# The MLP of a decoder layer by one level of Strassen's algorithm: 7 block products for 8, with the sums of weight blocks on GpSimd

## The chip, the cores and the metric

The kernel runs on one core of a Trainium2 chip. The time is device microseconds of one execution; the median of three runs of the kernel before is 1074.55 us (1074.43 to 1076.7). The engines are named as in the profile: PE multiplies matrices (PEld is its load of weights), DVE, ACT and POOL work element by element on 128 partitions, SP issues the DMAs. PE writes its results to PSUM; DVE, ACT and POOL keep theirs in SBUF.

## What is computed

One step of a two-branch decoder layer on 512 prompt tokens and 8 sample tokens. The change concerns its last part, the MLP and what surrounds it:

```
x = x + g1 * (merged @ w_out)                       # w_out: 1024 x 1024
h2 = rmsnorm(x, norm2_g) * (1 + sc2) + sh2
ff = square(relu(h2 @ w_ff1)) @ w_ff2               # w_ff1: 1024 x 4096, w_ff2: 4096 x 1024
x = x + g2 * ff
y = rmsnorm(x, final_norm_g)
```

Scale, shift and gate (sc2, sh2, g2) come from a conditioning vector; the prompt has one and each sample its own. Everything is float32.

## The kernel before

Activations lie as features x tokens: a tile is 128 features by T = 520 columns, 512 of the prompt and 8 of the samples, and its two halves of 260 columns (HALF) go to PE one after the other. A tile of weights is 1024 rows x 128 columns. PE's format fp32r carries fewer bits than float32, so every operand is split in two parts, hi and lo: ACT casts it to hi (L68 for weights, L146 for activations), and DVE subtracts hi from it, which gives lo (L69, L147). A product is then three: hi hi, hi lo and lo hi (`products`, L100, 128 x 128 weights and 260 columns each).

The MLP runs over two halves of 2048 inner features. In each half, 16 tiles of the first product (8 blocks of 128 input features, 3 parts, 2 halves of the tokens: 48 matmuls a tile) are evacuated by DVE and ACT, squared, split and kept; then 8 output tiles of the second product (16 blocks, 96 matmuls a tile) are added to x by DVE (`residual`). These are 2 x 16 x 48 + 2 x 8 x 96 = 3072 matmuls.

The second norm's root is not waited for: `out_proj` multiplies x by 1 + sc2 and splits it for each of the eight output tiles of w_out, and the products begin on that. The shifts ride along as ten more columns of the second half (260 + 10 = 270), and `norm2` computes the root of the mean square meanwhile; L891 multiplies the products by it as it reads them from PSUM. The last output tile is computed half by half of the tokens (`last_tile`), so that the final norm of the first half lies beside the products of the second.

The order on every engine is set by the tile framework's scheduler from priorities and its own estimates; each engine then takes its instructions in that order. A weight tile comes by one DMA of 512 KB from SP's queue into one of four buffers (`wst`), and is split two tiles ahead of its use (AHEAD). POOL has next to nothing to do in the MLP.

Of the kernel before, what the change touches and what calls it, by code (L numbers as in the profile page):

```python
# [22 lines left out]
C = 128          # HGRN2 chunk  # L23
# [9 lines left out]
MODK = 7         # the product behind which a conditioning tile's transposes come  # L33
LEAD = 4         # first conditioning tiles ahead of the normed input's
# [4 lines left out]
T2 = T + NM + 1  # columns with the shifts beside the activations  # L39
# [6 lines left out]
class Kernel:  # L46
# [6 lines left out]
    # ---- weights: a tile is 1024 rows x 128 columns, in two parts that fp32r carries exactly  # L53
# [21 lines left out]
    def take_w(self, key):  # L75
# [18 lines left out]
    def products(self, ps, w, a, first, last, extra=0, halves=(0, 1)):  # L94
        """ps += W^T a, for one 128 x 128 tile of W and one tile of a, both in two parts."""
        (wh, wl), (ah, al) = w, a
        for n, (x, y) in enumerate(((wh, ah), (wh, al), (wl, ah))):
            for s in halves:
                c = slice(s * HALF, (s + 1) * HALF + s * extra)
                self.last_product = self.nc.tensor.matmul(ps[:, s, :c.stop - c.start], x, y[:, c],  # L100
                                                          start=first and n == 0, stop=last and n == 2)

    def gemm(self, keys, acts, extra=0):
        """[128, 2, HALF (+ extra in the second)] of W^T act for one tile of 128 output features."""
        ps = self.pmm.tile([128, 2, 512], F32, name="mm")
        for q, key in enumerate(keys):
            hi, lo = self.take_w(key)
            for k in range(KO):
                n = q * KO + k
                self.products(ps, (hi[:, k], lo[:, k]), acts[n], n == 0, n == len(keys) * KO - 1, extra)  # L110
# [4 lines left out]
    # ---- ScalarE's tables: what needs the exponential's and the root's stays together between sigmoids  # L115
# [34 lines left out]
    def rsqrt_small(self, x, n, p=128, w=16):  # L150
        """x[p, n] ** -0.5 to float32's accuracy (x normal and positive)."""
# [12 lines left out]
    # ---- constants and parameters  # L164
# [36 lines left out]
    def transpose_in(self, out, rows, n):  # L201
        """rows [n, 128] -> out [128, n]"""
# [8 lines left out]
    def bounds(self):  # L211
        """What depends on parameters through the exponential: HGRN2's lower bounds, RG-LRU's decay rates."""
# [7 lines left out]
        # lower bounds: softmax and exclusive cumsum over the one layer  # L220
# [17 lines left out]
    def decays(self):  # L238
        """c8 = 8 softplus(-lam); log1p(e) = 2 atanh(e / (2 + e))"""
# [15 lines left out]
    def parameters_mod(self):  # L255
        """The norms' scales and the conditioning's bias (plus one where a scale comes of it)."""
# [44 lines left out]
    # ---- conditioning  # L301
# [9 lines left out]
    def cond(self):  # L311
        """silu of the conditioning rows, transposed, with room for 32 of them."""
# [56 lines left out]
    # ---- the input, its norm, and its transpose  # L369
# [8 lines left out]
    def norm_x(self):  # L378
# [3 lines left out]
        junk = lambda: self.pmm.tile([128, 2, 512], F32, name="mm").rearrange("p a b -> p (a b)")  # noqa: E731  # L382
# [20 lines left out]
    def transposed(self, k):  # L403
        """Columns k * 128 .. + 128 of the rows, transposed where they are."""
# [15 lines left out]
    def affine_split(self, k, prompt, sample):  # L420
        """The normed input's tile k times 1 + scale, plus the shift, in two parts."""
# [7 lines left out]
        v = lambda t: t[:, :L].rearrange("p (t f) -> p t f", f=128)  # noqa: E731  # L429
# [4 lines left out]
    # ---- HGRN2  # L434
# [9 lines left out]
    def head_f(self, h, ps):  # L444
        """f = max(lb, floor) + (1 - lb) sigmoid(fa), k = (1 - lb) sigmoid(-fa)"""
# [43 lines left out]
    def head_sample_v(self, h, v):  # L489
# [3 lines left out]
        vs = self.sm.tile([NB, 128], F32, name="vs")  # L493
# [8 lines left out]
    def head_sample(self, h, st, vb, fkq):  # L502
# [5 lines left out]
        # four samples' states at a time, each with all samples' queries in its own 32 columns of the array  # L508
# [4 lines left out]
        ev = self.sm.tile([128, 256], F32, name="sev")  # L513
# [7 lines left out]
    def head_prompt(self, h, f, X, q, v, og):  # L521
        nc = self.nc
        # values as [s, v]
# [6 lines left out]
        # levels: Q_b[t] = q_t * f's from the b-block's start to t, K_b[s] = k_s * f's after s to the block's end,  # L530
        # T_b = the product of f over each b-block; a pair in neighbouring blocks 2i, 2i + 1 is K_b . Q_b
# [4 lines left out]
        a32 = self.sm.tile([128, NC, 32], F32, name="a32")  # L536
# [10 lines left out]
        def view(t, first_q, first_k, step, n, b):  # L547
            """n blocks of b columns, step apart, of Q from first_q on and of K from first_k on"""
# [616 lines left out]
```

## Time and profile before

| | |
|---|---|
| median of three runs | 1074.55 us |
| profiled execution, first to last instruction (its span) | 1070.9 us |
| median of the runs less that span | 3.65 us |
| from the first product of w_ff1 to the last of w_ff2 | 681.8 to 1061.0 us of the span |
| matmuls there | 3072 of 10132 on PE |

The execution that was profiled has no time of its own beside its span, so what lies around the span is taken from the median. The profile gives the busy time of each engine, the same in 40 slices of the span, the chain of work that ended last, and groups of instructions by line: `L69 DVE TENSOR_TENSOR wlo<-wst,whi 128x1024 ... x152 | 185.6, 1221` is line 69 on DVE, with the tile it writes and those that it reads, 152 instructions, 185.6 us in all and 1221 ns of one.

### The profile page before, as it was taken

Reading aid. Unit: us, or ns where it says so; the run is one execution under the profiler, and the core shown is the slowest. Engines: PE = TensorE matmul, PEld = TensorE weight load, DVE = VectorE, ACT = ScalarE, POOL = GpSimd, SP = SyncE. Lnnn points to the kernel's source line nnn. Section 1 sums busy time; section 2 is a strip of 40 time slices with the busy share of each in tenths; the row PEclk is TensorE's granted clock in tenths of the full one; section 3 lists DMA queues with packets and bytes.
Section 4 is the critical chain, followed back from the end, with each engine's and each line's share of the span. In section 5 each row is a group of like instructions: output and inputs, shape, how many; then the busy total and the mean of one; then the engine's idle time right before and its main releaser. Section 6 shows DMA issues by size and latency. Waiting matters only on the chain.

```text
span 1070.9 us, 23934 instructions
## 1 busy us (share of the span) xinstructions
PE 1035.1 (97%) x10132; PEld 998.7 (93%) x10132; DVE 603.9 (56%) x1429; ACT 446.8 (42%) x897; POOL 25.6 (2%) x68
## 2 busy tenths in 40 slices
PE   3899999999999999989999999999999999999996
PEld 1799999999999999989999999999999999999996
DVE  6568678596786867464333346665542235554333
ACT  5445744663574364351222234444421124443332
POOL 2200000000000000110000000000000000000000
PEclk9999999999999999999999999999999999999999
DMA  9953444334333324695555573333323333332312
GB/s 278 252 170 101 121 123 125 111 121 141 107 120 113 110 92 142 186 281 165 160 158 160 158 210 86 92 90 89 94 84 99 85 94 93 86 96 82 96 44 80
DMA packets 239212, 136.34 MB, mean 127 GB/s; under 512 B 5214, under 2 KB 233750, under 8 KB 239098
## 3 DMA queue, kind: packets, MB, share of 16 engines
q1 hardware_dynamic: 237218, 129.75, 42.3%
q0 software_dynamic: 1888, 5.07, 1.5%
q8 instruction: 79, 1.29, 0.5%
q14 instruction: 27, 0.22, 0.1%
HBM read 123.61 MB, written 11.26 MB: 126 GB/s over the span
## 4 chain that ended last, share of the span: by engine, by line
PE 93%; SPq 3%; DMA 2%; ACT 1%; DVE 1%; issue 0%; ACTq 0%; DVEq 0%
PE mm L100 82%; PE ps L339 2%; SPq L1061 2%; PE pb L685 1%; DMA wst<-in_w_in_dram 1%; PE ps L544 1%; DMA wm<-in_w_mod_dram 1%; PE pt L628 1%; PE pt L617 1%; SPq L62 1%; PE ps L512 1%; PE pt L630 1%; PE ps L582 0%; PE pt L611 0%; DMA vd<-vs 0%
## 5 line engine op out<-in xcount | busy, mean ns | idle before, releaser
L100 PE MATMUL mm<-h,whi 128*128 128x260 f32 (+1 forms) x3072 | 518.2, 287 | 1.4 <-ACT X L120 1.4
L100 PEld LDWEIGHTS mm<-h,whi 128*128 128x128 f32 x3072 | 432.2, 190 | 7.2 <-issue 3.4
L100 PE MATMUL mm<-h,wlo 128*128 128x260 f32 (+1 forms) x1536 | 318.7, 287 | 0.0
L68 ACT CAST whi<-wst 128x1024 fp32r<-128x1024 f32 x152 | 159.3, 1048 | 333.8 <-PE mm L100 288.4
L69 DVE TENSOR_TENSOR wlo<-wst,whi 128x1024 fp32r<-128x1024 f32 x152 | 185.6, 1221 | 118.7 <-ACT whi L68 116.7
L100 PEld LDWEIGHTS mm<-h,wlo 128*128 128x128 f32 x1536 | 241.4, 190 | 1.7 <-issue 1.0
L100 PE MATMUL mm<-a,whi 128*128 128x260 f32 x1024 | 171.3, 286 | 0.0
L100 PEld LDWEIGHTS mm<-a,whi 128*128 128x128 f32 x1024 | 142.3, 189 | 1.6 <-issue 1.4
L100 PE MATMUL mm<-b,whi 128*128 128x260 f32 x768 | 125.0, 284 | 0.0
L100 PEld LDWEIGHTS mm<-b,whi 128*128 128x128 f32 x768 | 105.9, 189 | 1.6 <-issue 1.6
L100 PE MATMUL mm<-a,wlo 128*128 128x260 f32 x512 | 105.0, 283 | 0.0
L100 PEld LDWEIGHTS mm<-a,wlo 128*128 128x128 f32 x512 | 79.5, 188 | 0.2 <-issue 0.2
L100 PE MATMUL mm<-b,wlo 128*128 128x260 f32 x384 | 78.9, 284 | 0.0
L100 PEld LDWEIGHTS mm<-b,wlo 128*128 128x128 f32 x384 | 59.7, 188 | 0.0
L808 DVE SCALAR_TENSOR_TENSOR ma<-mm,modT,ma 128x260 f32<-128x260 f32 x23 | 11.2, 488 | 70.4 <-PE mm L100 66.0
L893 ACT ACTIVATE t<-t,fsh 128x512 f32<-128x512 f32 x32 | 23.0, 723 | 57.4 <-DVE t L891 57.4
L895 DVE TENSOR_TENSOR t<-t 128x520 f32<-128x520 f32 x32 | 22.3, 700 | 20.9 <-ACT t L894 20.9
L147 DVE TENSOR_TENSOR a<-t,a 128x520 fp32r<-128x520 f32 x32 | 21.9, 696 | 12.8 <-ACT a L146 12.8
L146 ACT CAST a<-t 128x520 fp32r<-128x520 f32 x32 | 19.6, 626 | 18.4 <-DVE t L895 10.0
L796 DVE TENSOR_TENSOR t<-mm,t 128x520 f32<-128x520 f32 x8 | 5.6, 699 | 37.0 <-PE ps L355 37.0
L147 DVE TENSOR_TENSOR b<-t,b 128x520 fp32r<-128x520 f32 x24 | 16.6, 699 | 14.1 <-ACT b L146 14.1
L359 DVE TENSOR_REDUCE mods<-ps 128x9 f32<-128x36 f32 x32 | 6.1, 190 | 32.6 <-PE ps L355 32.5
(301 smaller groups left out, 1008.5 us busy)
## 6 DMA issues: line engine op xcount, KB each, us to landing
wst<-in_w_in_dram SPq DMA_DIRECT2D x64, 512.0 KB
wst<-in_w_ff_dram SPq DMA_DIRECT2D x64, 512.0 KB
wst<-in_w_mod_dram SPq DMA_DIRECT2D x32, 512.0 KB
wm<-in_w_mod_dram SPq DMA_DIRECT2D x16, 512.0 KB
st<-in_state_hgrn_dram SPq DMA_DIRECT2D x8, 512.0 KB
vb<-vd SPq DMA_DIRECT2D x8, 512.0 KB
out_dram<-st SPq DMA_DIRECT2D x8, 512.0 KB
wst<-in_w_branch_a_dram SPq DMA_DIRECT2D x8, 512.0 KB
```

Source lines behind the costliest of these rows:

```text
L62: self.nc.sync.dma_start(st, src[r0:r0 + 1024, c0:c0 + 128].rearrange("(k p) n -> p k n", p=128))
L68: self.nc.scalar.copy(hi, st)
L69: self.nc.vector.tensor_tensor(lo, st, hi.bitcast(F32), OP.subtract)
L100: self.last_product = self.nc.tensor.matmul(ps[:, s, :c.stop - c.start], x, y[:, c], start=first and n == 0, stop=last and n == 2)
L146: self.nc.scalar.copy(hi, full)
L147: self.nc.vector.tensor_tensor(lo, full, hi.bitcast(F32), OP.subtract)
L339: nc.tensor.matmul(ps[r:r + 32, :n], self.cT[:, k, :], w[:, k, :], start=k < 4, stop=k >= KO - 4)
L512: nc.tensor.matmul(po[j:j + 32, c:c + 128], fkq[:, 2], st[:, b], start=True, stop=True)
L808: nc.vector.scalar_tensor_tensor(x[:, :HALF], ps[:, 0, :HALF], g[:, 0:1], x[:, :HALF], OP.mult, OP.add)
L893: nc.scalar.activation(t[:, :L], t[:, :L], AF.Relu, bias=sh[:, 0:1])
L895: nc.vector.tensor_tensor(t, t, t, OP.mult)
L1061: nc.sync.dma_start(raw[k][:, :, j * 128:(j + 1) * 128], w[r:r + 1024, c:c + 128].rearrange("(k p) n -> p k n", p=128))
```

## The change

An output block is two tiles of features by two halves of the tokens, a block of weights 128 x 128 pairs: for a weight matrix of 2 x 2 blocks W11, W12, W21, W22 (rows by columns) and activations of 2 x 2 blocks, Winograd's form of Strassen's algorithm needs 7 products of sums of blocks where the plain form needs 8. A unit is now a pair of output tiles (1024 x 256 weights, `st_pair`): seven jobs of 4 blocks x 3 parts = 12 matmuls of 260 columns, 84 in all. There are 4 quarters of 1024 inner features, each with 4 pairs of the first product and 4 of the second: 32 pairs.

- **Weights.** `st_load` brings a pair by two DMAs of 512 KB. `st_prep` forms the four sums of weight blocks on POOL (`st_sum`, 128 x 512 each) and splits all seven operands, six jobs ahead of PE (LEADB), ACT casting and DVE subtracting 128 x 512 at a time.
- **Products.** `st_job` accumulates in PSUM: D takes jobs 1, 6, 5 and 3 in turn, C takes 7 and 4, A takes 2. Between jobs, ACT copies D and C out (`snap`), since later sums need what they held.
- **First product.** `hidden` adds the snaps (DVE for the two blocks that come from PSUM, POOL for one), takes square(relu()), forms the four sums of activation blocks on POOL, and splits the seven forms (3 x 260 and 4 x 260 columns).
- **Second product.** `added` adds to x: two blocks by DVE from PSUM, four snaps by POOL.
- **The norm.** h2 is now formed in full ahead of the products (`normed`): x times the root, times 1 + sc2, plus sh2, four sums on POOL for each of the four pairs of tiles, seven forms split. `out_proj` no longer scales and splits.
- **The end.** The final norm works on pairs of tiles (`final_pair`); the last pair has its order of jobs set so that the first half of the tokens is ready before job 3 (`st_open`).

```diff
+    def st_open(self, specs):
...
+            if p and whole:
+                order = (1, 2, 7, 6, 4, 5)
+            elif spec[3]:
+                order = (1, 7, 6, 2, 5, 4)
+            else:
+                order = (1, 7, 6, 2, 4, 5)
+            jobs = [(p, j) for j in order]
+            if p and not whole:
+                jobs.insert(2, (p - 1, 3))
+            whole = spec[3]
+            if whole:
+                jobs.append((p, 3))
...
+    def st_sum(self, a, op, b):
+        t = self.sw.tile([128, 4, 128], F32, name="wsum", bufs=4)
+        self.nc.gpsimd.tensor_tensor(t, a, b, op)
+        return t
+
+    def st_prep(self, until):
...
+            if j == 7:
+                w = self.st_sum(x["11"], OP.subtract, x["21"])
+            elif j == 6:
+                x["s1"] = self.st_sum(x["21"], OP.add, x["22"])
+                w = self.st_sum(x["s1"], OP.subtract, x["11"])
+                x["s4"] = self.st_sum(x["12"], OP.subtract, w)
+            else:
+                w = x[{1: "11", 2: "12", 4: "22", 5: "s1", 3: "s4"}[j]]
+            hi = self.sw.tile([128, 4, 128], F32R, name="bh", bufs=7)
+            lo = self.sw.tile([128, 4, 128], F32R, name="bl", bufs=7)
+            nc.scalar.copy(hi, w)
+            nc.vector.tensor_tensor(lo, w, hi.bitcast(F32), OP.subtract)
...
+    def st_job(self):
...
+        bank = {1: "D", 7: "C", 2: "A"}.get(j)
+        if bank:
+            st[bank] = self.pst.tile([128, 512], F32, name=f"st{bank}", bufs=1 if bank == "A" else 2)
+        ps = st["A" if j == 2 else "C" if j in (7, 4) else "D"][:, :HALF]
+        (wh, wl), f = self.blocks.pop((p, j)), self.FORM[j]
+        for k, (ah, al) in enumerate(st["acts"]):
+            for n, (w, a) in enumerate(((wh, ah), (wh, al), (wl, ah))):
+                nc.tensor.matmul(ps, w[:, k], a[:, f], start=bool(bank) and k == 0 and n == 0, stop=k == 3 and n == 2,
+                                 skip_group_check=True)
...
+    def forms(self, hi, lo, src, a, b):
+        self.nc.scalar.copy(hi[:, a:b], src)
+        self.nc.vector.tensor_tensor(lo[:, a:b], src, hi[:, a:b].bitcast(F32), OP.subtract)
...
+    def normed(self):
...
+        def block(k, odd, half):
...
+            nc.vector.tensor_tensor(f, self.x[m][:, c], self.rs[half], OP.mult)
+            n = L - HALF if half else HALF
+            if half:
+                nc.vector.tensor_tensor(f[:, n:], f[:, n:], sc[:, 1:9], OP.mult)
+                nc.vector.tensor_tensor(f[:, n:], f[:, n:], sh[:, 1:9], OP.add)
+            nc.scalar.activation(f[:, :n], f[:, :n], AF.Identity, bias=sh[:, 0:1], scale=sc[:, 0:1])
...
+    def hidden(self, k, out):
...
+        def sink(j, ps):
+            if j in (1, 7, 6, 5):
+                s[j] = self.snap(ps, f"s{j}")
+            if j in (2, 4):
+                with self.urgent():
+                    nc.vector.tensor_tensor(f[:, j // 4], ps, s[1 if j == 2 else 6], OP.add)
+            if j == 5:
+                nc.gpsimd.tensor_tensor(f[:, 2], s[5], s[7], OP.add)
+            s[-j] = True
+            if j in (4, 5) and -4 in s and -5 in s:
+                nc.vector.scalar_tensor_tensor(v, v, 0.0, v, OP.max, OP.mult)
+                out.append(self.new_forms(self.ffp, f"ff{k}"))
+                self.forms(*out[k], v, 0, 3)
+            if j == 3:
+                with self.urgent():
+                    nc.scalar.activation(f[:, 3], ps, AF.Relu)
+                    nc.vector.tensor_tensor(f[:, 3], f[:, 3], f[:, 3], OP.mult)
+                t = self.misc.tile([128, 4, HALF], F32, name="t4", bufs=1)
+                for n, a, b in ((2, f[:, 2], f[:, 3]), (0, f[:, 3], f[:, 0]), (1, f[:, 2], t[:, 0]), (3, f[:, 1], t[:, 1])):
+                    nc.gpsimd.tensor_tensor(t[:, n], a, b, OP.subtract)
+                self.forms(*out[k], t, 3, 7)
...
+    def added(self, m, after=None):
...
+        def plus(t, c, part):
+            nc.gpsimd.tensor_tensor(x[t][:, c], x[t][:, c], part, OP.add)
```

Three places show how instructions move. POOL's last work in the kernel before is two small DMAs of results and two fills of 8 columns (`h` is the scaled input of the MLP):

```order
L772 DMA out_dram<-rows 3x1024
L772 DMA out_dram<-rows 8x1024
L772 DMA out_dram<-rows 16x1x64
L772 DMA out_dram<-rows 8x1024
L843 MEMSET h_8599 128x8
L843 MEMSET h_8600 128x8
```

In the changed kernel, this is POOL around one pair of the first product (`wsum` sums of weights, `f` blocks of square(relu()), `t` sums of them, `s` snaps):

```order
L1036 TENSOR_TENSOR f<-s_9556,s_9448 128x260
L909 TENSOR_TENSOR wsum<-wst 128x512
L1048 TENSOR_TENSOR t_9625<-f 128x260 x2
L909 TENSOR_TENSOR wsum<-wst 128x512
L1048 TENSOR_TENSOR t_9625<-f,t_9625 128x260
L909 TENSOR_TENSOR wsum<-wsum,wst 128x512
L1048 TENSOR_TENSOR t_9625<-f,t_9625 128x260
L909 TENSOR_TENSOR wsum<-wst,wsum 128x512
```

POOL goes from nothing to nine operations with two inputs each in a pair, in one queue with the weights' sums between those of the activations.

DVE in the first product of the kernel before, one tile of output features (`mm` in PSUM, `rs` the root, `fsh` the shifts):

```order
L891 TENSOR_TENSOR t<-mm,rs 128x520
L892 TENSOR_TENSOR t<-t,fsh 128x8
L895 TENSOR_TENSOR t<-t 128x520
L147 TENSOR_TENSOR a<-t,a 128x520
L69 TENSOR_TENSOR wlo<-wst,whi 128x1024
```

DVE in the changed kernel, around one pair (`bl` the lo part of a weight operand, `ff0l` and `ff1l` of the forms, `stA` and `stC` in PSUM):

```order
L1034 TENSOR_TENSOR f<-stA,s_9429 128x260
L1034 TENSOR_TENSOR f<-stC,s_9497 128x260
L932 TENSOR_TENSOR bl<-wsum,bh 128x512
L1045 TENSOR_TENSOR f<-f 128x260
L976 TENSOR_TENSOR ff0l<-t_9472,ff0h 128x1040
L1039 SCALAR_TENSOR_TENSOR f<-f 128x780
L932 TENSOR_TENSOR bl<-wsum,bh 128x512
L932 TENSOR_TENSOR bl<-wst,bh 128x512
L976 TENSOR_TENSOR ff1l<-f,ff1h 128x780
L932 TENSOR_TENSOR bl<-wsum,bh 128x512
L932 TENSOR_TENSOR bl<-wst,bh 128x512
L932 TENSOR_TENSOR bl<-wsum,bh 128x512
```

A pair (two tiles) had two `wlo` subtractions of 1024; it has seven `bl` of 512 now, and the forms are 7 x 260 columns where two tiles had 4 x 260.

DVE at the start of the MLP, before, from the split of the squares' sum (`sqs`) on:

```order
L147 TENSOR_TENSOR sqs<-sq,sqs 128x520
L69 TENSOR_TENSOR wlo<-wst,whi 128x1024
L876 RECIPROCAL rs<-rs 128x260 x2
L69 TENSOR_TENSOR wlo<-wst,whi 128x1024
L891 TENSOR_TENSOR t<-t,rs 128x520 x2
```

And now (`ma` is x, `ff0h` to `ff3h` hold h2 before the split, `h20l` is a lo part):

```order
L856 TENSOR_TENSOR sqs<-sq,sqs 128x520
L863 RECIPROCAL rs<-rs 128x260 x2
L994 TENSOR_TENSOR ff0h<-ma,rs 128x260
L994 TENSOR_TENSOR ff1h<-ma,rs 128x260
L994 TENSOR_TENSOR ff2h<-ma,rs 128x260
L994 TENSOR_TENSOR ff3h<-ma,rs 128x260
```

The next eight rows are the other twelve blocks in the same way, the last two of them below; then comes the first lo part:

```order
L994 TENSOR_TENSOR ff2h<-ma,rs 128x260 x2
L994 TENSOR_TENSOR ff3h<-ma,rs 128x260 x2
L976 TENSOR_TENSOR h20l<-ff0h,h20h 128x260
L997 TENSOR_TENSOR ff0h<-ff0h,modT 128x8
L976 TENSOR_TENSOR h21l<-ff1h,h21h 128x260
```

All sixteen multiplications by the root stand ahead of the first subtraction that a product waits for.

More of the change, by code (lines that the diff above doesn't have):

```diff
@@ new lines, in norm2 @@
+            nc.scalar.activation(self.rs[s], ps[:, :HALF], AF.Sqrt, bias=self.epsc, scale=1.0 / D)
+            nc.vector.reciprocal(self.rs[s], self.rs[s])
+    def st_open(self, specs):
+        self.specs = specs
+        self.jobs = []
+        whole = True
+        for p, spec in enumerate(specs):
+            if p and whole:
[10 more added lines that the diff above has]
+                jobs.append((p, 3))
+            self.jobs += jobs
+        self.jobs_prep = self.jobs_done = self.pairs_loaded = 0
+        self.raw, self.sums, self.blocks, self.pairs = {}, {}, {}, {}
@@ new lines, in st_pair, with snap @@
+    def st_pair(self, p, acts, sink):
+        self.pairs[p] = {"acts": acts, "sink": sink}
+        while self.jobs_done < len(self.jobs) and self.jobs[self.jobs_done] != (p + 1, 1):
+            self.st_job()
+    def snap(self, ps, tag, scale=None):
+        t = self.misc.tile([128, HALF], F32, name=tag, bufs=1)
+        with self.urgent():
+            if scale is None:
+                self.nc.scalar.copy(t, ps)
+            else:
+                self.nc.scalar.activation(t, ps, AF.Copy, scale=scale)
+        return t
@@ new lines, in mlp @@
+    def mlp(self):
+        nc, tc = self.nc, self.tc
+        self.close_pool()
+        self.early.close()
+        enter = self.ctx.enter_context
+        self.pst = enter(tc.tile_pool(name="pst", bufs=1, space=PSUM))
+        self.ffp = enter(tc.tile_pool(name="ffp", bufs=1, reuse_waits="tile"))
+        top = ExitStack()
+        self.h2p = top.enter_context(tc.tile_pool(name="h2p", bufs=1, reuse_waits="tile"))
+        h2 = self.normed()
+        p = 0
+        for q in range(4):
+            ff = []
+            for j in range(4):
+                self.st_pair(p, h2, self.hidden(j, ff))
+                p += 1
+            for m in range(4):
+                last = q == 3
+                if last and m == 0:
+                    self.final_open(top)
+                self.st_pair(p, ff, self.added(m, self.final_after(m) if last else None))
+                p += 1
@@ L1084, in begin @@
             self.mod(mk[k], raw.pop(k))
[L1085 to L1086 removed]
+        hi, lo = (self.act.tile([128, KO, T], F32R, tag="h", name="h", bufs=2) for _ in range(2))
+        self.h = [(hi[:, k], lo[:, k]) for k in range(KO)]
         pss = self.transposed_s()
```

330 lines of the change are left out of this document (197 added, 133 removed).

## The prediction

> **What bounds the kernel now.** I read the page first: busy shares, then the chain of waits.
>
> ```profile
> span 1070.9 us, 23934 instructions
> PE 1035.1 (97%) x10132; PEld 998.7 (93%) x10132; DVE 603.9 (56%) x1429; ACT 446.8 (42%) x897; POOL 25.6 (2%) x68
> PE 93%; SPq 3%; DMA 2%; ACT 1%; DVE 1%; issue 0%; ACTq 0%; DVEq 0%
> ```
>
> The chain that ended last runs over PE for 93% of the span: fewer matmuls are worth their time, as long as PE is not made to wait. The view by stretches, cut at the MLP's four parts (first product, second product, and both again), shows the stage (us of the stretch, then busy time of PE, PEld, DVE, ACT, POOL, the granted clock, the DMA share, GB/s):
>
> ```profile
> 681.80:777.40 95.60, 95.60 (x776) 95.60 (x775) 58.38 (x87) 44.04 (x85) 0.00 (x0) 1.00 0.31 89
> 777.40:869.80 92.40, 92.40 (x773) 92.40 (x772) 28.40 (x49) 18.57 (x21) 0.00 (x0) 1.00 0.32 92
> 869.80:965.00 95.20, 95.20 (x771) 95.20 (x771) 53.10 (x80) 39.67 (x77) 0.00 (x0) 1.00 0.32 89
> 965.00:1061.00 96.00, 95.94 (x803) 95.59 (x801) 34.07 (x65) 30.59 (x95) 0.00 (x0) 1.00 0.21 61
> ```
>
> PE never rests there, at a clock of 1.00. POOL does nothing. A part has 768 matmuls: 92.40 / 768 = 0.120 us for one of 260 columns. The whole takes 379.2 us.
>
> **What goes.** 32 pairs x 84 = 2688 matmuls at 0.120 us are 323 us. The final norm's transposes stay; they are the 3.6 us by which the fourth stretch exceeds the second. So PE's own work falls by 379.2 - 323.4 - 3.6 = 52 us, and with it the time if PE stays the bound. Consecutive matmuls into one bank of PSUM cost nothing: the last tile before already works so, at three in 0.36 us:
>
> ```profile
> 1060.05 0.41 PE L100 MATMUL mm<-b,whi 128*128 128x260 f32 x2
> 1060.42 0.41 PE L100 MATMUL mm<-b,whi 128*128 128x260 f32 x2
> ```
>
> One pair takes PE 84 x 0.120 = 10.1 us. Everything else must fit into that.
>
> **What comes on ACT and DVE.** The groups by line give durations (mean ns last before the bar that follows with the idle time), the timeline the pace of two in a row:
>
> ```profile
> L68 ACT CAST whi<-wst 128x1024 fp32r<-128x1024 f32 x152 | 159.3, 1048 | 333.8 <-PE mm L100 288.4
> L69 DVE TENSOR_TENSOR wlo<-wst,whi 128x1024 fp32r<-128x1024 f32 x152 | 185.6, 1221 | 118.7 <-ACT whi L68 116.7
> L146 ACT CAST a<-t 128x520 fp32r<-128x520 f32 x32 | 19.6, 626 | 18.4 <-DVE t L895 10.0
> L895 DVE TENSOR_TENSOR t<-t 128x520 f32<-128x520 f32 x32 | 22.3, 700 | 20.9 <-ACT t L894 20.9
> 700.36 1.31 DVE L895 TENSOR_TENSOR t<-t 128x520 f32<-128x520 f32 x2 [0.75 <-ACT t L894]
> ```
>
> DVE: (1221 - 700) / 504 = 1.03 ns an element. Two of 0.70 end after 1.31 us, so the second came 0.61 after the first. In a row, then, 260 columns take 0.34 us, 512 take 0.60, 780 take 0.88, 1040 take 1.15. A pair of the first product: seven `bl` 4.2, two of 780 1.8, one of 1040 1.15, one of 260 0.34, together 7.5 us, and two additions from PSUM 0.7: 8.2 of 10.1. A pair of the second product: 4.2, three reads of PSUM 1.1, small ones 0.6: 5.9. ACT is 0.84 ns an element by its two rows: about 7 us at most. Either fits alone, if narrowly. DMA brings the same bytes at a share of 0.3 and is costed at nothing; what hides it is the load of a whole pair ahead.
>
> **What comes on POOL, and whom it meets.** A pair has four sums of 512 and five of 260 columns in the first product, four and four in the second. The trace has no such operation. Its nearest rows, on the timeline:
>
> ```profile
> 34.69 0.20 POOL L426 TENSOR_TENSOR ht<-xhs,modT 128x8 f32<-128x8 f32 x1
> 51.98 0.29 POOL L1110 MEMSET fkq<- 128x96 f32 x2 [1.02 <-DVE h L432]
> 52.21 1.00 POOL L1113 MEMSET at<- 128x512 f32 x2
> ```
>
> A fill writes 416 more columns in (1.00 - 0.29) / 2 = 0.36 us, about 0.85 ns a column; a sum of 8 columns takes 0.20. Lower end: a sum costs one such pass, 0.62 us for 512 and 0.41 for 260. Upper end: a pass for each input and one for the output, 1.49 and 0.85. I take two passes, 1.05 and 0.63: two inputs have to be fetched, while the write may lie beside it, and the fill is the nearest row. Then POOL has 7.4 us in a pair of the first product and 6.7 in one of the second.
>
> [...]
>
> Alone, that fits too. But DVE and POOL are not independent:
>
> ```profile
> 32.46 1.30 DVE L432 TENSOR_TENSOR h<-ht,h 128x520 fp32r<-128x520 f32 x2
> 33.23 0.59 POOL L426 TENSOR_TENSOR ht<-xhs,modT 128x8 f32<-128x8 f32 x1 [0.71 <-DVE h L432]
> 34.76 0.70 DVE L432 TENSOR_TENSOR h<-ht,h 128x520 fp32r<-128x520 f32 x1
> 34.96 0.55 POOL L427 TENSOR_TENSOR ht<-ht,modT 128x8 f32<-128x8 f32 x1
> ```
>
> The same little sum that took 0.20 us takes 0.59 and 0.55 when DVE is in a subtraction of two SBUF tiles. It ends at 33.82 and 35.51; DVE ended at 33.76 and 35.46. POOL waited for DVE's end, twice, to 0.06 us. The other direction can't be read here, since POOL never ran longer than a few columns. I take it as the same: one of the two works, the other waits for its whole operation.
>
> [...]
>
> Then DVE's operations with two SBUF inputs and POOL's add up. With 0.05 us for each change of hands, two for each POOL operation:
> - first product: 7.5 + 7.4 + 0.9 = 15.8 us a pair,
> - second product: 4.3 + 6.7 + 0.8 = 11.8 us a pair.
>
> Both exceed 10.1. Queued behind a POOL sum is a `bl`, behind that on DVE's queue everything else, and PE waits for `bl`. 16 x 27.6 = 442 us where PE would need 323.
>
> **The start.** The products now wait for the norm.
>
> ```profile
> 685.25 0.61 ACT L856 CAST h<-t 128x520 fp32r<-128x520 f32 x1
> 686.77 0.70 DVE L147 TENSOR_TENSOR sqs<-sq,sqs 128x520 fp32r<-128x520 f32 x1
> 691.90 1.28 ACT L875 ACT_TABLE_LOAD   x1
> 693.19 0.84 ACT L875 ACTIVATE rs<-ps,epsc 128x260 f32<-128x260 f32 x2
> 693.70 3.42 DVE L876 RECIPROCAL rs<-rs 128x260 f32<-128x260 f32 x2 [1.12 <-ACT rs L875]
> ```
>
> `sqs` was ready at 687.5; without the scale and split of h some 1.2 earlier, 686.3. Four products 0.5, table 1.3, roots 0.8: 688.9. From there DVE has, by the order shown: reciprocals 3.4, sixteen blocks 5.4, sixteen small ones 1.6, forms 9.0 (twelve of 260, eight of 520), eight `bl` 4.8, one read of PSUM 0.4: 24.6 us. POOL has sixteen sums 10.1, four of weights 4.2, handovers 2: 16.3. Added up, the forms are complete at 688.9 + 40.9 = 730. By then the operands of two pairs are prepared (fourteen `bl`, eleven sums, about 21 us of the 442). The MLP's shared work ends at 730 + 442 - 21 = 1151.
>
> **Other ends.** At each of the four changes from the first to the second product, PE stands until the last pair's forms come, through ACT, DVE, four POOL sums, ACT and DVE; most of that is counted, and about 3 us (ACT's two casts and PE's restart, during which the pair's queues drain) are not: 12 us. After the last subtraction PE still has about two jobs: 3 us. Behind the last product there were
>
> ```profile
> 1059.37 1.58 PE mm L100 x13
> 1065.81 0.65 DVE rows L965
> ```
>
> 1070.9 - 1060.95 = 10 us, in the chain; three more squares of about 0.4 and a wider multiplication make it 11.5. Together 1151 + 12 + 3 + 11.5 = 1177.5 of span; with the 3.65 us around it, by which the median of the runs exceeds the profiled span, **1181 us**.
>
> With POOL's lower end a pair takes 12.9 and, PE bound, 10.1: 368 us, the forms complete at 725, about 1107 in all. With the upper end 18.6 and 14.5: 530 us, 735, about 1270.
>
> **The rivals.**
> - *No exclusion in DVE's direction (faster).* POOL is delayed by DVE, but DVE takes its turns as if POOL were not there. Then POOL's waiting fits beside DVE's work and PE bounds the pairs at 10.1. The start costs DVE's 24.6 from 688.9, to 713.5, when PE has some 7 of 224 jobs behind it: 323 - 10 = 313, plus 12 for the four changes, 3.6 of transposes, 11.5 at the end: 1054 of span, 1057 us. For it: every wait in the rows is POOL's. [...] It decides from the point where DVE plus POOL exceed 10.1 us a pair; if DVE does not wait, they needn't be added.
> - *Partial exclusion (slower).* POOL blocks DVE for its fetches alone, half its time: 12.1 and 10.1 a pair, 355 us, forms at 723, about 1095 us.
> - *The clock.* PE waits a third of each pair, and the clock that it is granted could fall to half: 20 us a pair would pass the 15.8, and the time 1370. Against it is the page's first slice:
>
> ```profile
> PE   3899999999999999989999999999999999999996
> PEclk9999999999999999999999999999999999999999
> ```
>
> PE was 3 tenths busy there, and the clock stayed at 9 tenths or more. That the change doesn't remove the matmuls is out: its order has 2688 of them.
>
> **How the numbers follow.** Exclusion in both directions has 0.68, with its own range 1107 to 1235 (POOL's upper end of three full passes is cut by a tenth of the case: reads and writes have overlapped on every engine above). Partial exclusion has 0.05, the clock 0.02, no exclusion 0.25, of which the part below 1052 is about 0.05. The likeliest gives 1181. The range of 8 in 10 has to include most of the faster case: 1052 to 1235, leaving out 0.05 below and about 0.1 above. Faster by over 0.2% (what a measurement of this kernel can tell from no change) is 0.24, within 0.2% 0.01, slower 0.75.
>
> **What the changed profile would show.** Right: in the stretches of the first product, PE busy some 6 tenths, DVE and POOL together filling them; `bl` well over its 0.60 to 0.69 us on average, since it includes waiting, and POOL's sums of 512 over 1.05; PE waiting for `bl`. POOL's price can be read from sums that meet no DVE operation. Wrong: `bl` at 0.7 us and PE 9 tenths busy after the start (no exclusion); or PE idle while both DVE and POOL are idle too, which would be a chain of dependences that I costed at 12 us. The start is right if the first product comes near 695 and the first pair ends near 730; the span beyond the MLP and its last 11.5 us should be as before.

## The result, and the profile after

The changed kernel takes 1138.76 us (median of four runs, 1138.55 to 1140.03), the one before 1074.49 us beside it: 1.0603 times as long, with a 95% interval of 1.0586 to 1.062. The forecast was slower, 1181 us, and a range of 1052 to 1235.

The page of the changed kernel, first its span and busy times, then the chain by engine, then four rows of the slices:

```profile
span 1136.8 us, 24348 instructions
PE 1023.0 (90%) x9748; PEld 970.1 (85%) x9748; DVE 829.5 (73%) x1625; ACT 546.9 (48%) x1130; POOL 398.4 (35%) x353
PE 11%; DVE 4%; POOL 3%; issue 3%; ACT 1%; DVEq 0%; POOLq 0%; ACTq 0%
...
PE   3999999999999999999999986879977987797785
...
DVE  6567778768688574633333479989998999799894
...
POOL 2200000000000001200000026779987988898791
PEclk9999999999999999999999995989988998998998
```

PE has 384 matmuls fewer and is no longer full: from the 25th slice on, where the MLP begins, the row that was all nines has mostly sevens and eights, while DVE stands mostly at nine and POOL, behind the start, at seven to nine. The chain now goes through three engines (its followed part covers less than a quarter of the span; before, PE alone had 93%).

The groups of the page with the most that is new, busy time, then mean ns of one:

```profile
L909 POOL TENSOR_TENSOR wsum<-wst 128x512 f32<-128x512 f32 x64 | 110.3, 1734 | 179.7 <-DMA wst<-in_w_ff_dram 173.4
L932 DVE TENSOR_TENSOR bl<-wsum,bh 128x512 fp32r<-128x512 f32 x128 | 147.3, 1160 | 6.1 <-ACT bh L931 5.2
L932 DVE TENSOR_TENSOR bl<-wst,bh 128x512 fp32r<-128x512 f32 x96 | 104.5, 1092 | 10.1 <-ACT bh L931 9.9
```

`bl`, whose shortest records in this run are 0.64 to 0.68 us, is recorded at 1.09 to 1.16 on average. That is the mark which the prediction named: waiting within the instruction, in DVE's direction.

The view by stretches, cut where PE begins job 2 of the first pair of the second product, and near the first product's begin (columns as before):

```profile
675.00:717.60 42.60, 27.26 (x125) 23.18 (x123) 38.61 (x70) 26.14 (x55) 22.29 (x21) 0.64 0.07 21
...
758.80:801.50 42.70, 39.48 (x285) 38.45 (x286) 38.54 (x50) 21.74 (x42) 37.34 (x29) 0.88 0.25 75
801.50:864.15 62.65, 50.16 (x390) 48.92 (x388) 55.70 (x60) 29.67 (x59) 53.11 (x41) 0.95 0.29 84
```

A quarter (8 pairs) takes 42.70 + 62.65 = 105.35 us, where 672 matmuls at 0.120 us would be 80.6. The two stretches aren't four pairs each: DVE and POOL work ahead of PE (41 POOL operations in the second, where four pairs have 36), so only the quarter is set against the sums below. The MLP lasts from 675.0 to 1124.7, 449.7 us against 379.2 before: 70.5 us more. Its start comes 6.8 us earlier than before, and the rest behind the last product is 12.1 us (9.9 before). 70.5 - 6.8 + 2.2 is the 65.9 by which the span grew.

### The profile page after: what moved, and what is told of

Same layout as the page of the kernel before. It is cut to its first block, busy times and chain, and to the rows that moved or that the text cites. A ratio compares the mean times of both kernels' runs of the same rounds, so it can differ in the third digit from the quotient of the medians.

```text
span 1136.8 us, 24348 instructions
## 1 busy us (share of the span) xinstructions
PE 1023.0 (90%) x9748; PEld 970.1 (85%) x9748; DVE 829.5 (73%) x1625; ACT 546.9 (48%) x1130; POOL 398.4 (35%) x353
## 5 line engine op out<-in xcount | busy, mean ns | idle before, releaser
L99 PE MATMUL mm<-h,whi 128*128 128x260 f32 x2048 | 345.8, 286 | 1.4 <-ACT X L119 1.4
L99 PEld LDWEIGHTS mm<-h,whi 128*128 128x128 f32 x2048 | 284.6, 188 | 7.4 <-issue 4.2
L99 PE MATMUL mm<-h,wlo 128*128 128x260 f32 x1024 | 211.7, 285 | 0.7 <-DVE wlo L69 0.6
L909 POOL TENSOR_TENSOR wsum<-wst 128x512 f32<-128x512 f32 x64 | 110.3, 1734 | 179.7 <-DMA wst<-in_w_ff_dram 173.4
L99 PEld LDWEIGHTS mm<-h,wlo 128*128 128x128 f32 x1024 | 159.1, 188 | 2.6 <-DVE wlo L69 1.1
L932 DVE TENSOR_TENSOR bl<-wsum,bh 128x512 fp32r<-128x512 f32 x128 | 147.3, 1160 | 6.1 <-ACT bh L931 5.2
L931 ACT CAST bh<-wsum 128x512 fp32r<-128x512 f32 x128 | 78.9, 619 | 85.9 <-PE stD L953 52.1
L932 DVE TENSOR_TENSOR bl<-wst,bh 128x512 fp32r<-128x512 f32 x96 | 104.5, 1092 | 10.1 <-ACT bh L931 9.9
L99 PE MATMUL mm<-a,whi 128*128 128x260 f32 x512 | 84.9, 285 | 0.0
L909 POOL TENSOR_TENSOR wsum<-wsum,wst 128x512 f32<-128x512 f32 x32 | 50.8, 1586 | 11.0 <-DVE bl L932 10.8
L99 PE MATMUL mm<-b,whi 128*128 128x260 f32 x256 | 41.9, 286 | 0.0
```

Source lines behind the costliest of these rows:

```text
L99: self.last_product = self.nc.tensor.matmul(ps[:, s, :HALF], x, y[:, s * HALF:(s + 1) * HALF], start=first and n == 0, stop=last and n == 2)
L909: self.nc.gpsimd.tensor_tensor(t, a, b, op)
L931: nc.scalar.copy(hi, w)
L932: nc.vector.tensor_tensor(lo, w, hi.bitcast(F32), OP.subtract)
```

## What one operation holds, read from the trace

Before the experiments, the exclusion itself can be read. On the timeline of the start (begin, duration), first two POOL sums of 260 columns that meet no DVE operation, then three that take turns with DVE operations of 520 columns:

```profile
692.88 0.74 POOL L1012 TENSOR_TENSOR ff1l<-ff1h 128x260 f32<-128x260 f32 x1
693.58 0.74 POOL L1008 TENSOR_TENSOR ff1l<-ff1h 128x260 f32<-128x260 f32 x1
694.28 1.19 POOL L1012 TENSOR_TENSOR ff2l<-ff2h 128x260 f32<-128x260 f32 x1
695.44 1.20 POOL L1013 TENSOR_TENSOR ff0l<-ff0h,ff0l 128x260 f32<-128x260 f32 x1
696.60 1.20 POOL L1008 TENSOR_TENSOR ff2l<-ff2h 128x260 f32<-128x260 f32 x1
...
694.80 1.23 DVE L976 TENSOR_TENSOR h21l<-ff1h,h21h 128x520 fp32r<-128x520 f32 x1
695.95 1.23 DVE L976 TENSOR_TENSOR h22l<-ff2h,h22h 128x520 fp32r<-128x520 f32 x1
```

POOL's sums start every 1.16 us, and one DVE operation lies in each turn. DVE takes 0.61 for its own (the pace of two in a row in the kernel before), so POOL keeps DVE off for 0.55 us (its hold, in what follows), 2.1 ns a column, although its sum of 260 columns is recorded at 0.74. For 512 columns that gives an estimate of 1.08 us; undisturbed, such a sum is recorded at 1.29, in the next rows. There is no time between the turns: 0.61 and 0.55 are all of 1.16.

The next four rows, from the first product, are two DVE operations that read PSUM, a POOL sum beside them, and a DVE operation with SBUF inputs alone:

```profile
758.38 0.74 POOL L1036 TENSOR_TENSOR f<-s,s 128x260 f32<-128x260 f32 x1
759.09 1.29 POOL L909 TENSOR_TENSOR wsum<-wsum,wst 128x512 f32<-128x512 f32 x1
...
758.34 0.43 DVE L1034 TENSOR_TENSOR f<-stA,s 128x260 f32<-128x260 f32 x1 [1.84 <-POOL t L1048]
758.69 0.42 DVE L1034 TENSOR_TENSOR f<-stC,s 128x260 f32<-128x260 f32 x1
759.21 2.00 DVE L1039 SCALAR_TENSOR_TENSOR f<-f 128x780 f32<-128x780 f32 x1
```

The two that read PSUM take 0.43 and 0.42 us, and POOL's beside them its undisturbed 0.74: neither waits. The third, 0.96 us on average in the runs below where POOL makes no sums of weights, takes 2.00, as a POOL sum of 512 columns had begun 0.12 before it. Its own 0.96 began at 760.25, then, which is 0.13 before POOL's recorded end (760.38). The same split shows in one small operation, x plus 8 columns, both in SBUF: before (no POOL work beside it) and in the changed kernel.

```profile
L812 DVE TENSOR_TENSOR ma<-ma,rst 128x8 f32<-128x8 f32 x23 | 3.6, 159 | 0.0
```

```profile
L1084 DVE TENSOR_TENSOR ma<-ma,rst 128x8 f32<-128x8 f32 x16 | 13.5, 842 | 0.0
```

## The experiments

Theory A: operations on DVE with two SBUF inputs and the time that POOL holds add up, as if both went through one port. "The port" is from here on a name for the exclusion that the rows above measure; no trace shows what in the chip it is. Rivals: the order of dependences through POOL's queue, the single `f`, the norm's start, the clock. Each time is a median; the kernel before, run again beside each group of experiments, took 1073.5 to 1073.9 us.

**Take the weight sums away.** Raw blocks stand for the sums, so their 128 POOL operations aren't done.

```diff
-                w = self.st_sum(x["11"], OP.subtract, x["21"])
+                w = x["11"]
...
-                x["s1"] = self.st_sum(x["21"], OP.add, x["22"])
-                w = self.st_sum(x["s1"], OP.subtract, x["11"])
-                x["s4"] = self.st_sum(x["12"], OP.subtract, w)
+                x["s1"] = x["21"]
+                w = x["22"]
+                x["s4"] = x["12"]
```

> The four sums of weight blocks are left out (raw blocks stand in their place), everything else stays: POOL keeps five sums of 260 columns in a pair of the first product and four in one of the second. Theory A (DVE operations with two SBUF inputs and POOL's reading sums exclude each other, and their sum sets the pace of a pair): in a pair of the first product 4 x 1.08 us of POOL's hold go, 15.6 becomes about 11, the second product's 10.7 becomes PE's 10.1; the time falls by some 85 us to 1045 to 1060, and the bl subtractions fall from 1.13 us towards 0.75. Theory B (the chain through the single buffers f and t4 sets the first product's pace, the exclusion only stretches operations that have room): 1100 to 1130. Theory C (POOL's queue itself is too slow): like A in time, but bl stays near 1.1 us.

Measured: 1069.87 us, 0.9968 (0.9958 to 0.9978) of the kernel before, 69 us less than the changed one. `bl` by line, and the two stretches of one quarter:

```profile
L932 DVE TENSOR_TENSOR bl<-wst,bh 128x512 fp32r<-128x512 f32 x224 | 185.3, 844 | 48.1 <-ACT bh L931 40.7
```

```profile
832.45:875.21 42.76, 40.87 (x322) 39.13 (x322) 32.96 (x58) 25.20 (x48) 18.63 (x20) 1.00 0.31 89
875.21:920.29 45.08, 42.62 (x353) 42.20 (x352) 34.56 (x52) 26.68 (x53) 16.43 (x17) 1.00 0.35 104
```

A quarter takes 87.8 us for 105.3. The sums of weights are what the change lost by. Without them it would be worth 0.3%, which is no more than the moved load gives by itself (last experiment): seven products for eight bought nothing. Theory A had expected 1045 to 1060 us, with PE as the bound at 80.6 a quarter: some 7 us of waits a quarter remain. `bl` fell, but to 0.84 and not to 0.75.

**Keep POOL's work and its place in the order, but let it read nothing.** Each sum is replaced by a fill of the same tile with a constant; the sums are left out.

```diff
-        self.nc.gpsimd.tensor_tensor(t, a, b, op)
+        self.nc.gpsimd.memset(t, 0.03)
```

> POOL writes each of the four weight-sum tiles with a fill instead of a sum (the sums are left out, the output has other numbers): POOL's operation stays, its reads go. Theory A in the form that only reads exclude: the fills take 0.53 us and do not touch DVE, bl about 0.75 us, time as without the sums, 1045 to 1060. Theory A' (any POOL operation excludes): 4 x 0.45 us of hold a pair stay, the first product about 12.6 a pair, time 1075 to 1090, bl about 0.9 us. Theory B: 1100 to 1130.

Measured: 1070.31 us, 0.9966 (0.9953 to 0.9978). Its groups on POOL and DVE:

```profile
L932 DVE TENSOR_TENSOR bl<-wsum,bh 128x512 fp32r<-128x512 f32 x128 | 106.6, 841 | 28.7 <-ACT bh L931 19.3
L909 POOL MEMSET wsum<- 128x512 f32 x128 | 66.6, 525 | 251.8 <-PE mm L99 132.6
L932 DVE TENSOR_TENSOR bl<-wst,bh 128x512 fp32r<-128x512 f32 x96 | 77.4, 810 | 22.4 <-ACT bh L931 21.4
```

The fills stand in the same queue, write the same tiles and are waited for by the same operations, `bl` stands at 0.84 and 0.81 us for 0.84 in the run without sums, and the time is that run's: what POOL writes doesn't keep DVE off. (The expected time was again 1045 to 1060 us, and missed by the same 10.) A fill (0.53 us) is shorter than a sum, so a share of the queue's own length isn't excluded by this run. As a bound by itself it is: a quarter's 32 sums of 512 columns and 36 of 260 take 68 us at their undisturbed 1.29 and 0.74, less than PE's 80.6.

**Do the same sums on DVE.** Nothing is left out.

```diff
-        self.nc.gpsimd.tensor_tensor(t, a, b, op)
+        self.nc.vector.tensor_tensor(t, a, b, op)
```

> The four weight sums go to DVE (0.60 us each instead of a hold of 1.08 on POOL); the activation sums stay on POOL. Theory A: the shared work of a pair falls from 14.5 to 12.7 in the first product and from 10.8 to 9 in the second, so PE's 10.1 bounds the second: time 1075 to 1100, faster than the changed kernel although DVE gets 2.4 us more a pair. Rival (POOL's sums cost DVE little, DVE's own 8.2 us a pair is what matters): DVE goes to 10.6 us a pair, over PE's 10.1, and the time stays or grows, 1135 to 1160. With A, bl falls towards 0.85 us.

Measured: 1107.69 us, 1.0319 (1.0302 to 1.0336) of before, and 31 us less than with POOL.

```profile
851.51:895.50 43.99, 42.65 (x321) 41.30 (x321) 41.11 (x68) 23.89 (x47) 21.07 (x19) 0.94 0.29 85
895.50:948.43 52.93, 44.58 (x355) 43.74 (x353) 44.56 (x74) 27.82 (x54) 22.58 (x17) 0.97 0.30 90
```

DVE has 128 operations more and the kernel is faster, which fits a sum that costs DVE 0.60 us on itself and 1.08 on POOL (estimates, the first from two operations of 520 columns that end 0.61 us apart, the second from the turns above): work given to an engine that was idle was dearer than the same work on the busy one. The gain is smaller than theory A's, which had 1075 to 1100 us; the table below shows where the sum of both engines' work puts this version.

**Two buffers for `f`.** In the changed kernel PE's largest wait (view of waits, 758 to 1074: total, times, longest) is this:

```profile
PE stA L953 <- DVE f L1034: 32.5, 10, 6.3
```

It says that PE waits for the single `f` to come free. With two:

```diff
-        s, f = {}, self.misc.tile([128, 4, HALF], F32, name="f", bufs=1)
+        s, f = {}, self.misc.tile([128, 4, HALF], F32, name="f", bufs=2)
```

> The changed kernel with two buffers for f in place of one (and for sq, which shares its place); nothing else of the MLP changes. Theory A (the port): a pair of the first product takes 14.5 us of DVE operations with two SBUF inputs plus POOL holds (7.5 + 4 x 1.08 + 5 x 0.55), whatever the buffers; 15.6 is measured now, so at most 1 us a pair goes: 1122 to 1139 us, and DVE's bl stay at 1.0 us or over. Rival B (a chain through the single f): PE and POOL wait for f's next round, and with two buffers the 40 us that PE's queue waited for f in the changed kernel's groups go: about 13 us a pair and 1097 us.

Measured: 1143.29 us, 1.0655 (1.0639 to 1.0671); 4.5 us worse than with one, and just outside the expected 1122 to 1139. (The run also gives `sq`, which shares the place of `f`, two buffers, and moves a few small tiles of the earlier stages to another pool.) The same view, of PE and of DVE:

```profile
PE stA L953 <- DVE bl L932: 13.9, 10, 2.6
PE stD L953 <- DVE bl L932: 6.6, 4, 3.4
PE stC L953 <- ACT ff2h L975: 6.1, 2, 3.1
```

```profile
DVE f L1039 <- POOL f L1036: 9.7, 8, 2.9
```

PE's wait for `f` is gone and others have come in its place; rival B, 1097 us, falls. The largest wait of the trace was a place where the port's delay came to light, not its cause.

**Take POOL out of DVE's way, step by step.** On top of the sums on DVE: the squares on ACT and `f`'s third block by DVE from PSUM (first); the four sums of `f` on DVE too (second); two buffers for `f` as well, with the same small moves as above (third).

```diff
-                nc.gpsimd.tensor_tensor(f[:, 2], s[5], s[7], OP.add)
+                with self.urgent():
+                    nc.vector.tensor_tensor(f[:, 2], ps, s[7], OP.add)
...
-                nc.vector.scalar_tensor_tensor(v, v, 0.0, v, OP.max, OP.mult)
+                nc.scalar.activation(v, v, AF.Relu)
+                nc.scalar.activation(v, v, AF.Square)
...
-                    nc.vector.tensor_tensor(f[:, 3], f[:, 3], f[:, 3], OP.mult)
+                    nc.scalar.activation(f[:, 3], f[:, 3], AF.Square)
...
-                    nc.gpsimd.tensor_tensor(t[:, n], a, b, OP.subtract)
+                    nc.vector.tensor_tensor(t[:, n], a, b, OP.subtract)
```

> The changed kernel with the weight sums on DVE, the squares on ACT (Relu, then Square) and f's third block added by DVE straight from PSUM; POOL keeps four subtractions of 260 columns in a pair of the first product. Theory A (the port): DVE 9.7 us (seven bl 4.2, four sums 2.4, 0.9, 1.15 and 1.05 for the rest) plus POOL 4 x 0.55 = 2.2: 11.9 a pair, where the kernel with only the sums on DVE took 13.2; 16 x 1.3 = 21 us less than its 1107.7: about 1087 us, slower than before. Rival B (a chain through the single f, not the port): no gain where the chain has the same links, 1100 to 1110 us.

> As v1, and the last four subtractions on DVE too, so that POOL shares nothing with DVE in the MLP. Theory A (the port): DVE 9.7 + 4 x 0.34 = 11.1 a pair of the first product, 13 us less than v1: about 1074 us, the same as before; bl falls to 0.7 to 0.85 us. Rival B (a chain through the single f): the same as v1 within 5 us.

> As v2, with two buffers for f. Theory A: DVE's 11.1 us a pair stay, 1069 to 1075 us. Rival B (the chain through the single f): PE's 10.1 becomes the bound of the first product and the time falls by 10 us or more against v2, to about 1060 us or less.

Measured: 1103.14 us (1.0281, 1.0264 to 1.0298), 1086.42 (1.0127, 1.0109 to 1.0145) and 1082.9 (1.0091, 1.0077 to 1.0106). Each step helps, but all three miss what theory A expected, by 16, 12 and 8 to 14 us. The first lies where rival B, a chain through the single `f`, had it (1100 to 1110 us). Its page shows POOL waiting for the last square, which is now on ACT:

```profile
L1050 POOL TENSOR_TENSOR t<-f 128x260 f32<-128x260 f32 x32 | 32.1, 1022 | 150.4 <-ACT f L1047 103.9
```

A longer way through `f` may have taken back what the lighter DVE gave; this wasn't tested. The second step gave 16.7 us, where rival B expected 5 at most. One quarter of the third:

```profile
788.70:878.55 89.85, 84.97 (x674) 82.64 (x673) 84.85 (x155) 57.50 (x108) 17.69 (x16) 0.98 0.32 95
```

My estimates had changed the first product alone. In the second, DVE's sums of weights stand beside reads of PSUM (1.9 us a pair) that could lie beside POOL's holds before and now add to DVE's own time. With these, DVE is busy for 84.85 of 89.85 us, and PE needs 80.6: two engines that both are nearly full. In a quarter DVE rests for 5 us, and PE takes 9 more than it needs. The table sets the sums of a quarter against the quarter measured. The lower end is what needs the port: in the changed kernel 7.5 + 4 x 1.08 + 5 x 0.55 = 14.6 us a pair of the first product and 4.3 + 4 x 1.08 + 4 x 0.55 = 10.8 of the second, four times; in the other versions with 0.60 for a sum of weights on DVE, without POOL's hold for it, and so on. The upper end has DVE's reads of PSUM (0.7 to 1.05, and 1.9 us a pair) added. In us:

| | DVE and POOL, lower to upper end | measured |
|---|---|---|
| changed kernel | 102 to 112 | 105.3 |
| weight sums on DVE | 86 to 97 | 96.9 |
| ... squares on ACT | 79 to 91 | 95.6 |
| ... sums of `f` on DVE | 76 to 88 | 90.8 |
| ... two buffers for `f` | 76 to 88 | 89.9 |
| weight sums left out | 67 to 77, and PE 80.6 | 87.8 |

Where the sum is far above PE's 80.6, the measured quarter lies within it; where the two come near each other, 2 to 7 us of waits remain on top of the larger, which I did not take apart further. So the rows of turns and the first three experiments carry theory A; the last steps don't tell its price from that of waits. The second buffer for `f` gave 3.5 us over the second step, between what A (next to nothing) and B (10 or more) expected: with the port free, the single `f` does have a small share.

**The start and the clock.** In the stretch 690 to 735 the changed kernel's matmuls ran at a granted clock of 0.77. Here 64 matmuls whose result isn't read stand behind the norm's two, so that PE doesn't rest.

```diff
+        spare = self.ppt.tile([128, 512], F32, name="pt")
+        for n in range(64):
+            nc.tensor.matmul(spare[:, :HALF], self.ones_r, parts[0][:, :HALF], start=n == 0, stop=n == 63)
```

> The changed kernel with 64 matmuls of 260 columns added behind the two that sum the norm's squares (their result is not read), so that PE works through the 8 to 10 us in which it waits for the first forms (64 x 0.120 = 7.7 us at full clock). If rest is what lowers the granted clock, the stretch 676 to 690, at 0.56 in the changed kernel, shows 0.9 or more. Theory A (forms bound the start: DVE and POOL share the port until 717): the time stays within 2 us of 1138.8, since PE waits for forms anyway. Rival B (the halved clock bounds the start, 0.217 us a matmul in place of 0.120): some 90 matmuls gain 0.097 each, 6 to 9 us: 1130 to 1133 us.

Measured: 1142.55 us, 1.064 (1.062 to 1.0659): not faster, 4 us slower. The timeline says why, the first product of its MLP being the last row:

```profile
679.56 4.33 PE L866 MATMUL pt<-sqs,ones_r 128*128 128x260 f32 x22
683.72 0.40 PE L861 MATMUL ps<-sqs,ones_r 128*128 128x260 f32 x2
...
689.79 0.50 PE L956 MATMUL stD<-h20h,bh 128*128 128x260 f32 x2 [0.63 <-ACT h20h L978]
```

The scheduler put 22 of the added matmuls ahead of the norm's second sum, which made the root late. In the changed kernel the first product was at 685.69, 4.10 earlier. Job 2 of the second product's first pair, without the added matmuls and with them:

```profile
758.82 0.39 PE L953 MATMUL stA<-ff0h,bh 128*128 128x260 f32 x1 [2.94 <-DVE f L1034]
```

```profile
762.96 0.39 PE L956 MATMUL stA<-ff0h,bh 128*128 128x260 f32 x1 [2.94 <-DVE f L1037]
```

That is 73.1 and 73.2 us behind the first product, and the 4 us by which theory A's 1138.8 is missed are the late root. So the start took the same time, at another clock: 690 to 735 had 0.77 and now 0.88 (below, the changed kernel first), and 676 to 690 had 0.56 and now 0.88.

```profile
690.00:735.00 45.00, 37.14 (x209) 33.70 (x209) 43.32 (x58) 25.69 (x55) 38.38 (x32) 0.77 0.15 47
```

```profile
690.00:735.00 45.00, 31.32 (x192) 27.49 (x191) 43.51 (x66) 27.28 (x59) 34.45 (x29) 0.88 0.12 36
```

DVE is full in both. The start is bound by the forms, and PE's slow clock lay beside its waiting. A second kernel with these matmuls is the third version above with the norm's sums on DVE too, four lines like this:

```diff
-            nc.gpsimd.tensor_tensor(t[:, 2], f[:, 2], f[:, 3], OP.subtract)
+            nc.vector.tensor_tensor(t[:, 2], f[:, 2], f[:, 3], OP.subtract)
```

> The version with the MLP's sums on DVE, the squares on ACT and two buffers for f (1082.9 us), and now the norm's sixteen sums of forms on DVE too, and the same 64 matmuls. Theory A: 16 x (0.55 - 0.34) = 3.4 us of DVE and port time less at the start: 1078 to 1081 us. Rival B (the clock bounds the start): 6 to 9 us less on top: 1070 to 1075 us, the same as before the change.

Measured: 1083.71 us, 1.01 (1.0082 to 1.0119), no better than 1082.9, and outside what both theory A and rival B expected. First product and job 2 of the second product's first pair, in the third version and in this one:

```profile
683.18 0.80 PE L953 MATMUL stD<-h20h,bh 128*128 128x260 f32 x2 [5.77 <-ACT h20h L975]
742.00 0.39 PE L953 MATMUL stA<-ff0h,bh 128*128 128x260 f32 x1
```

```profile
687.17 0.50 PE L956 MATMUL stD<-h20h,bh 128*128 128x260 f32 x2 [0.64 <-ACT h20h L978]
742.02 0.55 PE L956 MATMUL stA<-ff0h,bh 128*128 128x260 f32 x1 [0.67 <-DVE f L1037]
```

The first product is again 4.0 us late, and the way from there is 4.0 us shorter, near theory A's 3.4. But here the sums and the clock (0.92 for 0.88 between 690 and 735) changed together, so this run doesn't say which of them gave it. That the clock costs the start nothing rests on the first pair of kernels alone.

**What made the earlier stage 6.8 us shorter.** The kernel before issued the load of the final norm's gain from POOL's queue at 445.24, ahead of the branches' tiles. The issue, the wait for weights that follows in the chain, and the stretch behind it:

```profile
445.24 0.58 POOL L1127 DMA_DIRECT2D gbc<-in_final_norm_g_dram  x1 [392.04 <-ACT ma L120]
```

```profile
446.68 11.56 DMA wst<-in_w_in_dram
```

```profile
455.00:470.00 15.00, 12.27 (x108) 11.37 (x108) 7.78 (x15) 7.33 (x13) 3.76 (x7) 0.89 1.01 304
```

The DMA engines are full there, and PE is not. The change moved that load to the end. Doing this alone in the kernel before:

```diff
-        self.nc.gpsimd.dma_start(self.gbc, self.i["final_norm_g"].partition_broadcast(128))
...
+            self.nc.sync.dma_start(self.gbc, self.i["final_norm_g"].partition_broadcast(128))
```

> The kernel before with one part of the change alone: the broadcast load of the final norm's weights is issued by SP ahead of the final tiles, not by POOL ahead of the loads of the branches. If the 5 us that the changed kernel gains between 440 and 480 us of the span come from this load, the time falls by 3 to 6 us to 1069 to 1071 and PE's wait of about 3 us there is gone. If they come from the changed placement of pools and buffers, the time stays at 1074.

Measured: 1070.23 us, 0.9968 (0.9956 to 0.998), with this stretch:

```profile
455.00:470.00 15.00, 14.45 (x140) 13.55 (x139) 10.13 (x20) 10.20 (x19) 4.84 (x9) 1.00 1.00 301
```

About 3.6 us of the median is this load (3.0 by the first product of w_ff1, which comes at 678.78), about half of the 6.8; where the other half comes from was not tried. This small edit is also the version that beats both kernels, by 0.3% and 6%.

## Why the prediction was right

- **PE's work falls by 52 us: right in its count** (384 matmuls fewer), and worth nothing while PE waits. PE's need of 80.6 us a quarter was met by no version.
- **Exclusion in both directions (0.68): right.** In the kernel before only POOL is seen waiting for DVE; that DVE waits for POOL in the same way, and that its reads of PSUM stay out of the sums of 15.8 and 11.8 us a pair, was assumed, and no row showed it then. In the changed kernel an operation of 780 columns took 2.00 us for 0.96 beside a POOL sum, and the reads of PSUM took 0.43 and 0.42. The rows of turns show it, the reads of PSUM show its limit, and the runs with fills, with the sums left out and with the sums on DVE show that it is dear, though none gave all that was expected of it. The three rivals are out as they were stated: without exclusion in DVE's direction `bl` would stand at 0.7; with half of it, POOL would hold 0.37 of 0.74 and not 0.55; and the clock was 0.94 on average from 717.6 to 1124.7 (half, 0.50, came in single stretches of 5 us, as 760 to 765). But the prediction's "whole operation" isn't exact either: 0.55 of the recorded 0.74 is three quarters, a part of the way towards the partial exclusion.
- **The size, 1181 for 1139: 42 us too much.** 6.8 of them are the earlier stage, 5.6 the way from there to the last form, 28.9 the way from the last form to the last product, 1.7 what lies between span and median; the end gives 0.6 back. The quarters, which make the 28.9: the prediction's 4 x 27.6 + 3 is 113.4 us and 105.3 was measured. Its handovers of 0.9 and 0.8 us a pair, 6.8 a quarter, don't exist; and POOL's holds, taken as 1.05 and 0.63, are 1.08 and 0.55, 1.9 us less a quarter. The price that I took for POOL's duration was wrong (1.29 and 0.74 are recorded, below its upper end of 1.49 and 0.85; that reads and writes overlap on every engine, for which a tenth of the case was cut from that end, no run shows). That it came near what counts is luck: it was built from passes of a fill, and a sum keeps DVE off for less than its record. The four changes and other waits, 3 us a quarter in the prediction, are about 4: 105.3 less the 101.6 of the account's lower end.
- **The start: too long.** The last form was expected 48.2 us behind the last product of w_out and came 42.6 behind it (717.6), for the same handovers and holds; the first product came at 685.7 instead of "near 695", because the earlier stage ended 6.8 us sooner, which the prediction had not seen in the moved load, and because the first two matmuls need only hi parts, which ACT makes while DVE still multiplies. The third had to wait for the lo part, as forecast from the order, and came at 689.63:

```profile
685.69 0.80 PE L953 MATMUL stD<-h20h,bh 128*128 128x260 f32 x2 [5.58 <-ACT h20h L975]
689.63 0.59 PE L953 MATMUL stD<-h20l,bh 128*128 128x260 f32 x1 [3.13 <-DVE h20l L976]
```

- **The end** was forecast at 11.5 us and is 12.1.
- **"PE busy some 6 tenths"** is a miss: it shows 8 in the first product's stretch (50.16 of 62.65). That stretch holds 390 matmuls, more than the 336 of four pairs: 46.8 us at 0.120 each, and an estimate of 49 at its clock of 0.95.

## What to carry to other kernels

An idle engine was not free here: before work is moved to POOL, count the operations with two SBUF inputs on DVE in that stage, and add POOL's two-input sums to them at the 2.1 ns a column of this case; a DVE operation that reads PSUM (0.43 and 0.42 us here, beside a POOL sum at its 0.74), and a POOL fill (`bl` at 0.84 and 0.81 here, as without POOL's sums), need not be added. If the sum exceeds the bound engine's time, the same operation on DVE itself can be cheaper: here, by 31 us for 128 sums. And a wait that heads the list is worth an experiment before it is called a cause: here it went, and the time did not fall.

## What the runs showed that I had not expected

- A POOL sum of 260 columns keeps DVE off for 0.19 us less than the profile records for it, so the undisturbed duration overstates what DVE loses (0.74 for 0.55).
- PE's clock was low behind the pause of 5.6 us ahead of the first product (0.50 between 684 and 692; with the added matmuls, 676 to 690 had 0.88 for 0.56), where matmuls came 0.217 us apart for 0.120, and stayed low while its jobs came singly: 0.64 over the first 42.6 us of the MLP in the stretches above. In the start it cost nothing that could be measured, as DVE was the bound there; what the 0.88 to 0.95 of the later stretches cost was not tried.
- A load of the gain vector, moved out of a stretch with full DMA engines, was worth 0.3% by itself.
